# The row sum of two weight blocks, made by an adding DMA instead of VectorE, in a seven-product encoder layer

## The chip, the cores and the metric

The kernel runs on one core of a Trainium2 chip. The metric is the device time of one execution in microseconds: the median of three runs, 1981.27 us (1980.73 to 1982.22) for the kernel before. "Groups" below are the seven-product groups of the two large linear layers, and names such as B11 or T1 are the program's.

## The reference

One layer of an encoder over 512 tokens of width 2048, in float32:

```python
h = layer_norm(x, ln_in_g, ln_in_b)
z = h @ w_in
y = concat(attention(z), gelu(gate) * bidirectional_rg_lru(conv(z))) @ w_out
h = layer_norm(ALPHA * h + y, ln1_g, ln1_b)
f = square(relu(h @ w_up)) @ w_down          # 2048 -> 8192 -> 2048
h = layer_norm(ALPHA * h + f, ln2_g, ln2_b)
```

The change lies in the last two matrix products, `h @ w_up` and `... @ w_down`.

## The kernel before, in words

Every float32 operand is split into a high part (written as float32r by ScalarE, lines 121 and 159) and a low part (what is left, a subtraction on VectorE, lines 124 and 160). A product is then three matmuls: weight high by operand high, weight high by operand low, weight low by operand high.

The kernel goes through its stages in this order: the first norm and `w_in`, the attention and the recurrent branch, `w_out` with its norm, then `w_up` (from about 658 us on) and `w_down` (from about 1290 us on). For `w_up` and `w_down` the activations are cut into a 2x2 grid of blocks, and from the blocks seven operands are prepared once for a whole stage (B11, T3, T1, X4, B21, B22, T2), each with a high and a low part that stay in SBUF. The weights come as slabs of 128x1024 float32 (512 KB). Four slabs are the blocks a11, a12, a21, a22 of one group, and `winograd` (line 878) computes the group's four output blocks with seven block products instead of eight. The products run in the order B11, T3, T1, X4, B21, B22, T2, with 24 matmuls (3 for each of 8 slices) to each.

What the weights need ahead of a product: B11 takes a11, X4 takes a22 and B21 takes a12 as loaded; T3 takes a11-a21, T1 takes a21+a22, T2 takes a22 less that, and B22 takes a12 less T2's. These four sums are made by VectorE at line 876 (`tt`), each on 128x1024 float32 and each in place of one of its inputs. After that `wsplit` (line 839) makes the high part in one of three tiles `whi` and the low part in one of three tiles `wlo`.

The order of the instructions on each engine is set by a scheduler at build time, from the order in the program and its priorities: loads and splits are moved ahead of the products (the splits by `tc.high_priority`, line 841). Each engine then runs its own list in order. The loads are all issued by SyncE (SP) from one list; raw slabs go to seven buffers, of which the last four (`ws_p`, line 835) lie in space that is free only once the norm's rows R (`r_p`, freed at line 834) have been read for the last time, by the split of X4 in lines 826 to 833.

There are 57 groups: 30 in `w_up` (lines 924 to 936, after four blocks of 128 columns that are computed in the ordinary way) and 27 in `w_down` (lines 982 to 1016). `w_down` runs in four chunks, and at the end of `w_up` and of the first three chunks the operands of the next chunk are loaded from DRAM (`u_load`, line 912) and split; in between stands one block in the ordinary way (`classic`, line 760).

In the lists below, `raw` is a weight slab, `s` with a number the tiles s1 and s7, `st_mm`, `st_sc` and `st_tr` the PSUM banks of the products, `uo` an output tile of `w_up`, `R` the rows of a norm.

Of the kernel before, what the change touches and what calls it, by code (L numbers as in the profile page):

```python
# [9 lines left out]
F32 = mybir.dt.float32  # L10
# [3 lines left out]
ALU = mybir.AluOpType  # L14
# [4 lines left out]
P = 128  # L19
# [29 lines left out]
def body(tc, x, pos, vecs, consts, w_in, w_uq, w_kn, w_v, w_rg, w_out, w_up, w_down, out):  # L49
    nc = tc.nc  # L50
    V, A, T, G = nc.vector, nc.scalar, nc.tensor, nc.gpsimd
# [472 lines left out]
    for step, what in enumerate(ORDER):  # L524
        c, k = what[0], int(what[1])
# [309 lines left out]
    ws_p = pool("ws")  # L835
# [3 lines left out]
    def wsplit(f, n):  # L839
        woff[0] = (32, 0) if n in ("T3", "T1") else FAR  # L840
        with tc.high_priority(offset=PO2):
            w = wsplit_(f)
        woff[0] = FAR
        return w

    def wsplit_(f):
        hi = wtile(wr, "whi", 3)
        lon[0] += 1
        lo = wtile(wr, "wlo", 2) if lon[0] % 3 else wtile(ws_p, "wlo", 1)
        split(f, hi, lo)  # L850
        return hi, lo

    def wraw(k):
        if k % 7 < 3:
            return wr.tile([P, 1024], F32, tag="raw", name="raw", bufs=3)
        return ws_p.tile([P, 1024], F32, tag="raw", name="raw", bufs=4)
# [3 lines left out]
    def wload(src):  # L860
        t = wraw(rawn[0])
        rawn[0] += 1
        nc.sync.dma_start(out=t, in_=src)
        return t

    def product(acc, w, n, first):
        wh, wl = w
        sk = dict(skip_group_check=not first)
        for j in range(8):
            ws = slice(j * P, (j + 1) * P)  # L870
            T.matmul(acc, wh[:, ws], oph[n][:, j], start=first and j == 0, stop=False, **sk)  # L871
            T.matmul(acc, wh[:, ws], opl[n][:, j], start=False, stop=False, **sk)  # L872
            T.matmul(acc, wl[:, ws], oph[n][:, j], start=False, stop=j == 7, **sk)  # L873

    def tt(o, x, y, op):
        V.tensor_tensor(out=o, in0=x, in1=y, op=op)  # L876

    def winograd(slabs, evac, hook=lambda n: None):

        a11 = wload(slabs[0])  # L880
        a21 = wload(slabs[2])
        a22 = wload(slabs[3])
        a12 = wload(slabs[1])
        bank = lambda tag, bufs: ps.tile([P, HS], F32, tag=tag, name="st_" + tag, bufs=bufs)
        half = lambda n: ws_p.tile([P, HS], F32, tag=n, name=n, bufs=2)
        a, b, c, d = bank("mm", 3), bank("sc", 2), bank("tr", 3), bank("mm", 3)
        s1, s7 = half("s1"), half("s7")
        product(a, wsplit(a11, "B11"), "B11", True)
        hook("B11")
        A.activation(s1, a, AF.Copy)  # L890
        tt(a11, a11, a21, ALU.subtract)
        product(b, wsplit(a11, "T3"), "T3", True)
        A.activation(s7, b, AF.Copy)  # L893
        tt(a21, a21, a22, ALU.add)
        product(c, wsplit(a21, "T1"), "T1", True)
        tt(s7, s7, c, ALU.add)
        product(b, wsplit(a22, "X4"), "X4", False)
        hook("X4")
        tt(a11, a22, a11, ALU.subtract)
        product(a, wsplit(a12, "B21"), "B21", False)  # L900
        hook("B21")
        evac("c11", a, None)
        tt(a12, a12, a11, ALU.subtract)
        product(c, wsplit(a12, "B22"), "B22", False)
        hook("B22")
        product(d, wsplit(a11, "T2"), "T2", True)
        tt(s1, s1, d, ALU.add)
        evac("c21", s1, b)
        evac("c12", s1, c)
        evac("c22", s1, s7)  # L910
# [13 lines left out]
    for ch in range(NCL, DFF // 256):  # L924
        o = o_tile()

        def evac(which, x, y):
            t = o[:, 2 * int(which[1]) + int(which[2]) - 3, :]
            if y is not None:
                tt(t, x, y, ALU.add)  # L930
                x = t
            A.activation(t, x, AF.Relu)
            A.activation(t, t, AF.Square)
        winograd([w_up[4 * ch + i] for i in range(4)], evac,
                 *([next_ops(0)] if ch == DFF // 256 - 1 else ()))
        up_out(ch, o)
# [46 lines left out]
    for c in range(NCH):  # L983
        if c == 0:
            r_init(0)
        for i in range(KT // 2):
            sl = [w_down[(c * KT + 2 * i) * 2 + q] for q in range(4)]
            if c == NCH - 1 and i == KT // 2 - 1:
                last_pair(sl)
            elif i < NCL2:  # L990
                def evac(n, acc):
                    tt(r[2 * i + n], r[2 * i + n], acc, ALU.add)
                classic(sl, evac, [lambda n=n: u_load(c, n, n) for n in ("T3", "T1", "T2")] if i == 0 else ())
                if i == NCL2 - 1:
                    u_load(c, "T4", "X4")
            else:
                q = rp[i]

                def evac(which, x, y):
                    t = q[:, 2 * int(which[1]) + int(which[2]) - 3, :]  # L1000
                    if which == "c11":
                        tt(t, t, x, ALU.add)
                    elif which == "c22":
                        tt(y, y, x, ALU.add)
                        tt(t, t, y, ALU.add)
                    else:
                        tt(t, t, y, ALU.add)
                        tt(t, t, x, ALU.add)
                def prev_stats(n, i=i):
                    if n == "X4" and i == KT // 2 - 2:  # L1010
                        u_load(c, "B12", "X4")
                    if n == "B21":
                        for k in (2 * i - 2, 2 * i - 1):
                            to_tokens(r[k], st2, k)
                hook = () if c + 1 < NCH and i < KT // 2 - 1 else \
                    (next_ops(c + 1),) if c + 1 < NCH else (prev_stats,)
                winograd(sl, evac, *hook)
# [69 lines left out]
```

## Time and profile before

| | |
|---|---|
| median of three runs | 1981.27 us |
| the profiled execution | 1981.16 us |
| its span, from the first to the last instruction | 1979.4 us |
| mean granted TensorE clock | 0.998 |
| TensorE busy (matmul) | 1932.1 us, 98% |
| VectorE busy | 1501.8 us, 76% |
| ScalarE busy | 1014.6 us, 51% |
| GpSimd busy | 18.1 us, 1% |
| HBM | read 234.19 MB, written 46.14 MB |

The profiled execution is 0.11 us below the median, and 1.76 us of it lie outside its span. A busy share is an average over all stages; what limits one stage is read from the rows of that stage. "Idle before, releaser" tells how long an engine stood still ahead of an instruction, and which work ended last before it could start. The landing time of a DMA runs from its issue to its completion.

### The profile page before, as it was taken

How to read it: one execution, taken by the hardware profiler on the slowest of the kernel's cores; microseconds unless marked ns; L12 is line 12 of the kernel's file. 1: busy time of each engine (PE TensorE's matmuls, PEld its weight loads, DVE VectorE, ACT ScalarE, POOL GpSimd, SP SyncE). 2: the span in 40 equal slices, each digit the busy share in tenths (PEclk: the TensorE clock that was granted, in tenths of full speed). 3: DMA queues.
4: the chain of work that ended last, by engine and by line, in shares of the span. 5: the costliest groups of instructions: out<-in, count | busy, mean ns of one | idle time of the engine just before them, and what ended most of it. 6: DMA issues, size and time to landing. Idle time of an engine off the chain costs nothing.

```text
span 1979.4 us, 39294 instructions
## 1 busy us (share of the span) xinstructions
PE 1932.1 (98%) x16472; PEld 1899.7 (96%) x16472; DVE 1501.8 (76%) x2151; ACT 1014.6 (51%) x1479; POOL 18.1 (1%) x20
## 2 busy tenths in 40 slices
PE   6999999999999999999999999999999999999997
PEld 6999999888999999999999999999999999999997
DVE  7666655677433598888888888888898888888895
ACT  6565566555222455555555555566464454445453
POOL 1000000000000000000000000000000000000001
PEclk9999999999999999999999999999999999999999
DMA  7222222221333345454444445486364355347332
GB/s 244 96 96 94 91 93 85 65 59 65 107 107 123 115 150 204 156 180 154 179 159 162 176 156 182 153 295 223 118 222 162 107 185 198 109 140 244 100 104 86
DMA packets 113890, 284.19 MB, mean 144 GB/s; under 512 B 10161, under 2 KB 56369, under 8 KB 109617
## 3 DMA queue, kind: packets, MB, share of 16 engines
q1 hardware_dynamic: 113712, 281.68, 41.4%
q8 instruction: 129, 2.11, 0.4%
q14 instruction: 49, 0.39, 0.1%
HBM read 234.19 MB, written 46.14 MB: 142 GB/s over the span
## 4 chain that ended last, share of the span: by engine, by line
PE 88%; DVE 4%; ACT 3%; DMA 2%; issue 2%; POOL 0%; SPq 0%; ACTq 0%; DVEq 0%; POOLq 0%
PE st_mm L871 8%; PE st_mm L872 8%; PE st_mm L873 8%; PE mm L142 7%; PE mm L141 7%; PE mm L140 7%; PE st_tr L873 5%; PE st_sc L873 5%; PE st_sc L871 5%; PE st_tr L872 5%; PE st_tr L871 5%; PE st_sc L872 5%; PE mm L756 1%; PE mm L758 1%; PE mm L757 1%
## 5 line engine op out<-in xcount | busy, mean ns | idle before, releaser
L159 ACT ACTIVATE whi<-raw 128x1024 fp32r<-128x1024 f32 x399 | 423.5, 1063 | 513.5 <-DVE raw L876 251.6
L160 DVE TENSOR_TENSOR wlo<-raw,whi 128x1024 fp32r<-128x1024 f32 x399 | 484.5, 1222 | 129.4 <-ACT whi L159 123.5
L876 DVE TENSOR_TENSOR raw<-raw 128x1024 f32<-128x1024 f32 x228 | 278.3, 1221 | 3.6
L124 DVE TENSOR_TENSOR wlo<-raw,whi 128x1024 fp32r<-128x1024 f32 (+1 forms) x128 | 141.3, 1105 | 160.9 <-PE mm L142 110.3
L121 ACT ACTIVATE whi<-raw 128x1024 fp32r<-128x1024 f32 (+1 forms) x128 | 123.0, 966 | 195.6 <-PE mm L141 160.8
L141 PE MATMUL mm<-hl,whi 128*128 128x256 f32 x704 | 195.3, 277 | 0.0
L142 PE MATMUL mm<-hh,wlo 128*128 128x256 f32 x704 | 195.0, 277 | 0.0
L140 PE MATMUL mm<-hh,whi 128*128 128x256 f32 x704 | 194.7, 277 | 0.1
L140 PEld LDWEIGHTS mm<-hh,whi 128*128 128x128 f32 x704 | 132.2, 188 | 0.3 <-ACT xp L443 0.3
L142 PEld LDWEIGHTS mm<-hh,wlo 128*128 128x128 f32 x704 | 132.2, 188 | 0.1
L141 PEld LDWEIGHTS mm<-hl,whi 128*128 128x128 f32 x704 | 132.2, 188 | 0.0
L871 PE MATMUL st_sc<-X4h,whi 128*128 128x256 f32 x456 | 126.6, 278 | 2.0 <-ACT s L893 2.0
L873 PE MATMUL st_sc<-T3h,wlo 128*128 128x256 f32 x456 | 126.5, 277 | 1.8 <-DVE wlo L160 1.8
L871 PE MATMUL st_tr<-B22h,whi 128*128 128x256 f32 x456 | 126.6, 278 | 1.0 <-ACT whi L159 1.0
L873 PE MATMUL st_tr<-B22h,wlo 128*128 128x256 f32 x456 | 126.2, 277 | 0.7 <-DVE wlo L160 0.7
L871 PE MATMUL st_mm<-B21h,whi 128*128 128x256 f32 x456 | 126.0, 276 | 0.8 <-ACT s L890 0.8
L871 PE MATMUL st_mm<-T2h,whi 128*128 128x256 f32 x456 | 126.0, 276 | 0.4 <-ACT whi L159 0.4
L872 PE MATMUL st_sc<-X4l,whi 128*128 128x256 f32 x456 | 126.3, 277 | 0.0
L873 PE MATMUL st_sc<-X4h,wlo 128*128 128x256 f32 x456 | 126.2, 277 | 0.0
L871 PE MATMUL st_sc<-T3h,whi 128*128 128x256 f32 x456 | 126.1, 277 | 0.0
L872 PE MATMUL st_sc<-T3l,whi 128*128 128x256 f32 x456 | 126.1, 277 | 0.0
L873 PE MATMUL st_mm<-B11h,wlo 128*128 128x256 f32 x456 | 126.0, 276 | 0.0
(443 smaller groups left out, 6462.3 us busy)
## 6 DMA issues: line engine op xcount, KB each, us to landing
raw<-in_w_up SPq DMA_DIRECT2D x128, 512.0 KB, 3.3
raw<-in_w_down SPq DMA_DIRECT2D x128, 512.0 KB, 3.6
u_dram<-uo SPq DMA_DIRECT2D x32, 1024.0 KB, 3.8
raw<-in_w_in SPq DMA_DIRECT2D x50, 512.0 KB, 3.2
raw<-in_w_out SPq DMA_DIRECT2D x32, 512.0 KB, 3.2
X4l<-u_dram SPq DMA_DIRECT2D x18, 512.0 KB, 5.3
x<-in_x SPq DMA_DIRECT2D x8, 512.0 KB, 7.1
h_dram<-hf SPq DMA_DIRECT2D x32, 128.0 KB, 2.1
```

The source lines that it names most:

```text
L121: A.activation(hi[:, :w], raw[:, :w], AF.Copy)
L124: V.tensor_tensor(out=lo[:, :w], in0=raw[:, :w], in1=hi[:, :w].bitcast(F32), op=ALU.subtract)
L140: T.matmul(acc[:, c], wh, xh[:, c], start=first and t == 0, stop=False)
L141: T.matmul(acc[:, c], wh, xl[:, c], start=False, stop=False)
L142: T.matmul(acc[:, c], wl, xh[:, c], start=False, stop=last and t == 1)
L159: A.activation(hi, f, AF.Copy)
L160: V.tensor_tensor(out=lo, in0=f, in1=hi.bitcast(F32), op=ALU.subtract)
L756: T.matmul(o, wh[:, ws], oph[b][:, j], start=first and t == 0, stop=False)
L871: T.matmul(acc, wh[:, ws], oph[n][:, j], start=first and j == 0, stop=False, **sk)
L872: T.matmul(acc, wh[:, ws], opl[n][:, j], start=False, stop=False, **sk)
L873: T.matmul(acc, wl[:, ws], oph[n][:, j], start=False, stop=j == 7, **sk)
L876: V.tensor_tensor(out=o, in0=x, in1=y, op=op)
```

## The change

T1's sum a21+a22 is no longer made by VectorE. Each group gets a tile `s1w` of its own (two buffers, in `ws_p`): a plain DMA issued by SP loads a21 into it a second time, then an adding DMA issued by GpSimd (`accum_op=ALU.add`) adds a22 to it from DRAM. T1's split reads `s1w`. a21 and a22 are still loaded as before, for T3 and X4. The last line cuts the space that is kept for GpSimd's DMA descriptors to 8192 bytes a partition, which makes room for `s1w`.

```diff
@@ -881,6 +881,9 @@
         a21 = wload(slabs[2])
         a22 = wload(slabs[3])
         a12 = wload(slabs[1])
+        s1w = ws_p.tile([P, 1024], F32, tag="s1w", name="s1w", bufs=2)
+        nc.sync.dma_start(out=s1w, in_=slabs[2])
+        G.dma_start(out=s1w, in_=slabs[3], accum_op=ALU.add)
         bank = lambda tag, bufs: ps.tile([P, HS], F32, tag=tag, name="st_" + tag, bufs=bufs)
...
         A.activation(s7, b, AF.Copy)
-        tt(a21, a21, a22, ALU.add)
-        product(c, wsplit(a21, "T1"), "T1", True)
+        product(c, wsplit(s1w, "T1"), "T1", True)
@@ -1075,7 +1077,7 @@
-    nc = _bacc.Bacc("TRN2", target_bir_lowering=False, num_devices=1)
+    nc = _bacc.Bacc("TRN2", target_bir_lowering=False, num_devices=1, dynamic_dma_scratch_size=8192)
```

The scheduler lays the instructions out anew. Three places matter below.

SP's list of DMAs at the first group. Before (raw_8782, raw_8784, raw_8786 and raw_8788 are a11, a21, a22 and a12 of the first group, raw_9016 to raw_9022 those of the second):

```order
L863 DMA raw_8786<-in_w_up 128x1024
L777 DMA u_dram0_72<-uo_8307 128x2048
L863 DMA raw_8788<-in_w_up 128x1024
L863 DMA raw_9016<-in_w_up 128x1024
L863 DMA raw_9018<-in_w_up 128x1024
L863 DMA raw_9020<-in_w_up 128x1024
L863 DMA raw_9022<-in_w_up 128x1024
L863 DMA raw_9250<-in_w_up 128x1024
L777 DMA u_dram0_72<-uo_8308 128x2048
```

Now (raw_9018 to raw_9024 are the second group's, s1w_8790, s1w_9026 and s1w_9262 belong to the first, second and third group):

```order
L863 DMA raw_8786<-in_w_up 128x1024
L777 DMA u_dram0_72<-uo_8307 128x2048
L863 DMA raw_8788<-in_w_up 128x1024
L885 DMA s1w_8790<-in_w_up 128x1024
L863 DMA raw_9018<-in_w_up 128x1024
L863 DMA raw_9020<-in_w_up 128x1024
L777 DMA u_dram0_72<-uo_8308 128x2048
L863 DMA raw_9022<-in_w_up 128x1024
L863 DMA raw_9024<-in_w_up 128x1024
L885 DMA s1w_9026<-in_w_up 128x1024
L863 DMA raw_9254<-in_w_up 128x1024
L885 DMA s1w_9262<-in_w_up 128x1024
```

The first group's `s1w` stands right behind its a12, whose buffer is the first in `ws_p`, and ahead of the second group's slabs. On GpSimd, 57 adding DMAs stand in a row, one for each group, with nothing between them.

ScalarE's list at the first group. Before (whi_8826 is the high part for T3, whi_8856 that for T1, whi_8885 that for X4):

```order
L159 ACTIVATE whi_8826<-raw_8782 128x1024
L159 ACTIVATE whi_8856<-raw_8784 128x1024
L781 ACTIVATE uo_8308<-mm_8638 128x512
L782 ACTIVATE uo_8308<-uo_8308 128x512
L159 ACTIVATE whi_8885<-raw_8786 128x1024
L890 ACTIVATE s1_8794<-st_mm_8790 128x256
L159 ACTIVATE whi_8914<-raw_8788 128x1024
L893 ACTIVATE s7_8795<-st_sc_8791 128x256
```

Now (whi_8829 is the high part for T3, whi_8858 that for T1, whi_8887 that for X4):

```order
L159 ACTIVATE whi_8829<-raw_8782 128x1024
L781 ACTIVATE uo_8308<-mm_8638 128x512
L782 ACTIVATE uo_8308<-uo_8308 128x512
L893 ACTIVATE s1_8797<-st_mm_8793 128x256
L896 ACTIVATE s7_8798<-st_sc_8794 128x256
L159 ACTIVATE whi_8858<-s1w_8790 128x1024
L159 ACTIVATE whi_8887<-raw_8786 128x1024
L159 ACTIVATE whi_8916<-raw_8788 128x1024
```

T1's high part has moved behind the two copies of PSUM banks, and X4's and B21's high parts stand behind it.

TensorE's list where T1's product of the first group begins, now:

```order
L873 MATMUL st_sc<-T3h,wlo 128x256
L871 MATMUL st_tr<-T1h,whi 128x256
L872 MATMUL st_tr<-T1l,whi 128x256
L871 MATMUL st_sc<-X4h,whi 128x256
L872 MATMUL st_sc<-X4l,whi 128x256
L873 MATMUL st_tr<-T1h,wlo 128x256
L871 MATMUL st_tr<-T1h,whi 128x256
```

Before, X4's two matmuls stood behind all 24 of T1. This is the only place in the whole list of TensorE where the order has changed.

## Rows read from the trace of the kernel before

**Rows 1.** The page's busy times, and its group of VectorE's sums.

```profile
PE 1932.1 (98%) x16472; PEld 1899.7 (96%) x16472; DVE 1501.8 (76%) x2151; ACT 1014.6 (51%) x1479; POOL 18.1 (1%) x20
...
L876 DVE TENSOR_TENSOR raw<-raw 128x1024 f32<-128x1024 f32 x228 | 278.3, 1221 | 3.6
```

**Rows 2.** Busy time by stretch: w_up's groups, then the passage to w_down.

```profile
core 0: us, PE busy (x) PEld busy (x) DVE busy (x) ACT busy (x) POOL busy (x), PEclk, DMA share, GB/s
750.00:1298.00 548.00, 548.00 (x4828) 548.00 (x4827) 458.57 (x544) 297.31 (x483) 0.00 (x0) 1.00 0.47 167
1298.00:1326.00 28.00, 25.80 (x222) 25.19 (x221) 26.07 (x31) 23.30 (x31) 0.00 (x0) 1.00 1.01 351
```

**Rows 3.** TensorE's waits from 1298 to 1950: us in total, times, longest.

```profile
PE st_sc L871 <- ACT s L893: 2.0, 3, 1.2
PE st_sc L873 <- DVE wlo L160: 1.8, 2, 1.0
PE st_tr L871 <- ACT whi L159: 1.0, 1, 1.0
PE st_mm L871 <- ACT s L890: 0.8, 1, 0.8
PE st_tr L873 <- DVE wlo L160: 0.7, 2, 0.4
PE st_mm L871 <- ACT whi L159: 0.4, 1, 0.4
PE mm L758 <- DVE wlo L124: 0.3, 1, 0.3
```

**Rows 4.** VectorE in a later group: T1's low part.

```profile
1011.70 1.22 DVE L160 TENSOR_TENSOR wlo<-raw,whi 128x1024 fp32r<-128x1024 f32 x1
```

**Rows 5.** ScalarE in the group of rows 4: T1's high part.

```profile
1009.71 1.06 ACT L159 ACTIVATE whi<-raw 128x1024 fp32r<-128x1024 f32 x1 [0.65 <-PE st_mm L872]
```

**Rows 6.** ScalarE one group on: T1's high part.

```profile
1028.79 1.06 ACT L159 ACTIVATE whi<-raw 128x1024 fp32r<-128x1024 f32 x1 [0.65 <-PE st_mm L872]
```

**Rows 7.** Landing of all 228 loads of line 863.

```profile
DMA to landing us min/median/max: 3.0/3.3/9.1
```

**Rows 8.** VectorE in order of time: last read of R, first group's sums.

```profile
739.33 1.22 DVE L160 TENSOR_TENSOR X4l<-R,X4h 128x1024 fp32r<-128x1024 f32 x1
740.47 2.47 DVE L876 TENSOR_TENSOR raw<-raw 128x1024 f32<-128x1024 f32 x2
```

**Rows 9.** Line 863, issues at 740.6 and 741.0 us: first and last, their landing.

```profile
L863 SPq DMA_DIRECT2D raw<-in_w_up x2: 328/376/425, 740.6 to 741.0; - x2
...
DMA to landing us min/median/max: 3.7/4.1/4.6
```

**Rows 10.** ScalarE in order of time: T1's high part in the first group.

```profile
743.04 1.06 ACT L159 ACTIVATE whi<-raw 128x1024 fp32r<-128x1024 f32 x1 [0.25 <-DVE raw L876]
```

**Rows 11.** TensorE in order of time: T1's first matmul in the first group.

```profile
747.96 0.28 PE L871 MATMUL st_tr<-T1h,whi 128*128 128x256 f32 x1
```

**Rows 12.** GpSimd's groups: count, busy us and mean ns of one, idle before.

```profile
L409 POOL TENSOR_TENSOR sp_d<-sp_c,sp_b 128x16 f32<-128x16 f32 x1 | 2.9, 2930 | 1.9 <-DVE sp_b L406 1.9
L292 POOL TENSOR_TENSOR rsx<-vex,mhalf 128x1 f32<-128x1 f32 x4 | 2.2, 552 | 31.0 <-DVE vex L290 23.6 <-DVE sp_d L417 7.4
```

**Rows 13.** Landing of line 863's load issued at 745.4 us.

```profile
DMA to landing us min/median/max: 5.3/5.3/5.3
```

**Rows 14.** Landing of line 777's store of 1 MB issued at 749.0 us.

```profile
DMA to landing us min/median/max: 7.6/7.6/7.6
```

**Rows 15.** TensorE near the end: the first matmul after a wait.

```profile
1967.77 0.47 PE L217 MATMUL trb<-ident,R 128*128 128x128 f32 x1 [3.54 <-ACT R L199]
```

**Rows 16.** Stretches of 1 us near the end, columns as in rows 2.

```profile
1966.00:1967.00 1.00, 0.00 (x0) 0.00 (x0) 0.29 (x2) 0.09 (x1) 0.90 (x2) 0.69 0.00 0
1967.00:1968.00 1.00, 0.23 (x1) 0.23 (x2) 1.00 (x3) 0.72 (x1) 1.00 (x1) 0.50 0.00 0
...
1972.00:1973.00 1.00, 1.00 (x6) 0.75 (x4) 0.69 (x2) 0.62 (x2) 1.00 (x1) 0.50 0.75 263
1973.00:1974.00 1.00, 0.24 (x2) 0.12 (x2) 0.76 (x2) 0.56 (x1) 0.23 (x1) 0.89 0.75 262
```

## The prediction

> **What bounds the kernel now.** I began with the page's busy times: TensorE works for 98% of the span and VectorE for 76% [rows 1]. That is an average, so the next view is the table by stretch. In the 548 us of `w_up`'s groups TensorE is busy for all 548.00 us, while VectorE works 458.57 us, 84% [rows 2]. In that stretch no work taken off VectorE can end anything sooner; TensorE's list sets the time. The reader should look for the places where TensorE does wait. From 1298 to 1950 us there are 7.0 us of waits in seven rows [rows 3], nearly all where `w_down`'s chunks change: there the DMA share stands at 1.01 and the granted clock at 1.00 [rows 2]. Only three of these rows, 1.8 + 0.7 + 0.3 = 2.8 us, end with work of VectorE [rows 3]. So the change can win at most a few microseconds, and the question is what its new chain costs where the chain has no lead.
>
> **What is removed.** One of four sums per group: 57 of the 228 sums of 1221 ns, 69.6 us of VectorE [rows 1]. In the groups of `w_up` it lies beside a TensorE that never waits: worth nothing. At the changes of chunk it can be worth at most the 2.8 us that end on VectorE. I take 0: in those 28 us ScalarE is busy 23.30 and the DMA share is 1.01 [rows 2], so when VectorE comes sooner, ScalarE or a landing is late next.
>
> **What is added.** Per group one plain load of 512 KB from SP and one adding DMA of 512 KB from GpSimd. VectorE's sum had no load of its own; the new chain is load, then adding DMA, then T1's split. There are two buffers `s1w`, so a group's load can start when T1's split of two groups before is done.
>
> In the running state that is early enough. T1's low part ends at 1011.70 + 1.22 = 1012.92 us [rows 4]; T1's high part comes every 1028.79 - 1009.71 = 19.08 us [rows 6, 5], so two groups on it is due at 1047.87. That leaves 34.9 us for load and addition. A load lands in 3.3 us at the median and 9.1 at the longest [rows 7]. Even two of the longest fit, with 16 us to spare: cost 0. Behind GpSimd's wait nothing is queued but the next group's addition, and on SP the load's wait for the split two groups back has passed before its turn. The traffic grows from a DMA share of 0.47 [rows 2] by two more transfers of 512 KB on the six such units of a group (four slabs and a 1 MB store), or three if the adding one also reads its destination: 0.47 x 8/6 = 0.63 to 0.47 x 9/6 = 0.71, below 1.
>
> In the first group there is no lead. `s1w` lies in the space of R, which VectorE reads until 739.33 + 1.22 = 740.55 us [rows 8]. SP can issue only then; before, it issued a12 at 740.6 and the next slab at 741.0, and that second one landed 4.6 us later, at 745.6 [rows 9]. In the new order that second place is `s1w`'s. Before, T1's sum was one of two made from 740.47 on [rows 8], its high part began at 743.04 [rows 10], and TensorE reached T1 at 747.96 [rows 11].
>
> Now the addition starts at 745.6 at the earliest. No row shows an adding DMA or a DMA from GpSimd, so it is bounded. Below: GpSimd takes no time and the transfer is the shortest load, 3.0 us [rows 7]: sum ready at L = 748.6. Above: GpSimd takes its longest instruction, 2.9 us [rows 12], and the transfer the longest load, 9.1 us [rows 7]: L = 757.6. A gain is excluded, since T1 had its inputs in time before. Nearest are the transfers issued in this same crowded stretch: a load of 512 KB took 5.3 us [rows 13], a store of 1 MB 7.6 us [rows 14]. The adding DMA writes 512 KB but must also read both addends, so I take a value between them, 6.4 us, and 0.6 us for GpSimd, its short instruction [rows 12]: L = 745.6 + 0.6 + 6.4 = 752.6.
>
> From L on: the high part, 1.06 us [rows 10], then the low part, 1.22 us [rows 4]; so all of T1 can run from L + 2.28. ScalarE's X4 split is queued behind T1's, so X4 cannot fill the gap. TensorE's new order lets four matmuls go early; each takes 548.00/4828 = 0.113 us [rows 2], 0.45 in all. TensorE loses L + 2.28 - 747.96 - 0.45 = L - 746.13: **6.5 us** at my L, 2.5 and 11.5 at the ends. After it TensorE is the bound again, so nothing gives this back. The second group's sum has the same chain but is due 19.08 us later, plus the loss; its load is issued behind the 1 MB store, which was issued at 749.0 and landed at 756.6 [rows 14]; a load and an addition of 3.3 us each would end at 763.2, and T1's split is due at 743.04 + 19.08 + 6.5 = 768.6 [rows 5, 6, 10].
>
> **The clock.** Near the end TensorE waits 3.54 us until 1967.77 [rows 15]. The granted clock falls to 0.69 in the microsecond before and stands at 0.50, the 1.2 GHz level, until 1973, when it is 0.89 [rows 16]. From 1967.77 to 1973.1 that is 5.3 us at half speed, a loss of 2.7 us. The wait in the first group would be 752.6 + 1.06 - 747.96 = 5.7 us, longer than this one. I add **2.7 us**; the lower end is 0, if the wait turns out short.
>
> **The passages.** At the later changes of chunk one `s1w` load stands between two operand loads. At 351 GB/s [rows 2] its 512 KB take 1.5 us, three times, 4.5 us if all of it reached TensorE. The operand loaded there is X4, the fourth of the next group's products, so I take 0. The shift of SBUF addresses has no row that prices it; the matmuls of all seven products run at one rate, so I take 0.
>
> **Sum.** 0 + 6.5 + 2.7 + 0 = +9.2 us on the profiled 1981.16 gives 1990.4. That execution lies 0.11 below the median of the runs, so against the median the forecast is **1990.5 us**, +0.46%. A measurement of this kernel can tell about 0.2% from no change, which is 4.0 us.
>
> **Rivals.** The wait is short: no change. If the addition lands like the shortest load, L = 748.6, TensorE loses 2.5 us, its wait is 748.6 + 1.06 - 747.96 = 1.7 us, shorter than the one near the end, and I leave the clock's price out: 1983.8. For it: the median load is 3.3 us [rows 7]. Against it: every transfer issued at this moment took 3.7 us or more [rows 9, 13, 14]. The Trainium skill, page "DMA: Bandwidth & Descriptors", section "Anatomy of one DMA — SWDGE (gpsimd) path", prices a DMA from GpSimd at about 2.0 us plus bytes / 436e3; my estimate from it is 3.2 us for 512 KB, with which the sum would be +2.7 us, this rival's side. No run here shows such a DMA yet. Chance 0.26.
>
> The passages gain: faster. If VectorE's shorter list pulls the work that ends all the waits at the changes of chunk forward, 7.0 us go [rows 3]; with the short wait the net is 2.5 - 7.0 = -4.5 us, 1976.8. It decides only if more than 2.5 + 4.0 = 6.5 of the 7.0 us vanish. Against it: only 2.8 us of them end on VectorE. Chance 0.05.
>
> Every group is late: much slower. If load and addition take longer than 34.9 us, T1 waits in each of the 57 groups: each microsecond over is 57 us, 2038 at the first. Nothing in the rows comes near; only the unknown speed of the addition speaks for it. Chance 0.07.
>
> The passages lose. The 4.5 us above on top of the forecast: 1995.0. Chance 0.04.
>
> That VectorE keeps the sum can be excluded: its list has one sum less in each group, and the adding DMAs stand on GpSimd's.
>
> **How the numbers follow.** The forecast itself (a wait of more than 4 us net, in the first group) gets 0.58. Slower is this, every group late and the passages losing: 0.58 + 0.07 + 0.04 = 0.69. Within 0.2% is the short wait, 0.26; faster 0.05. The range begins at 1982.0, the short wait's 1983.8 with 1.8 us of VectorE's waits gone [rows 3], and ends at 1997.0, the upper L with the clock, 1981.3 + 11.5 + 2.7 = 1995.5, and one passage's 1.5 us. Left out are every group late and most of the gain: some 0.12, with the tails under 0.2.
>
> **What would show it.** Right: in the first group a wait of TensorE ahead of T1's first matmul of some 5.7 us (near 748 to 754), which ends with ScalarE's high part and behind it the adding DMA; some microseconds of granted clock 0.50 after it; TensorE busy again in all of the rest of `w_up`; VectorE's sums at 171 instead of 228. Wrong: a landing of the first addition before 750.2 us, where the loss falls to 4 us; a wait ahead of T1 in later groups; a stretch from 1298 on with clearly fewer or more waits than 7.0 us; no fall of the clock.

## The result and the profile after

The changed kernel takes **2002.53 us** (median of four runs, 2001.94 to 2003.18) where the kernel before takes 1981.54 on the same chip: ratio 1.0097, 95% interval 1.0085 to 1.0109, 21 us slower. The forecast was 1990.5, range 1982.0 to 1997.0: the right side and less than half of the size. The profiled execution has a span of 2000.2 us, 20.8 more than before.

The page of the changed kernel: busy times of the engines, VectorE's sums, and the two DMA queues (packets, MB, share of 16 engines' span; q1 is SP's, q0 is GpSimd's).

```profile
PE 1939.1 (97%) x16472; PEld 1905.9 (95%) x16472; DVE 1447.9 (72%) x2094; ACT 1015.2 (51%) x1479; POOL 68.1 (3%) x77
...
L876 DVE TENSOR_TENSOR raw<-raw 128x1024 f32<-128x1024 f32 x171 | 209.0, 1222 | 4.2
...
q1 hardware_dynamic: 121920, 311.57, 45.2%
q0 software_dynamic: 8208, 29.89, 9.1%
```

VectorE has lost its 57 sums (228 to 171, [rows 1]) and TensorE works as many matmuls as before, 7 us longer. Where did 21 us go? The start of each group's first matmul (B11) in the two traces, taken group by group (counted from 0), gives it: the difference grows in three places and is nearly flat between them. I call that growth, between a group's start and the next one's, the **loss** of the group:

| place | near | loss, us |
|---|---|---|
| group 0, the first of `w_up` | 748 | 11.1 |
| groups 1 to 28 | 772 to 1306 | 0.0 |
| group 31, the second behind the passage to `w_down` | 1378 | 4.9 |
| group 51, the first behind the last change of chunk | 1834 | 5.2 |
| all the rest together (most of it: group 37, +0.8, and group 30, -0.4) | | 0.2 |

TensorE's time line of the changed kernel at the three places; the bracket is the wait ahead of the matmul and what ended it.

```profile
755.48 0.58 PE L871 MATMUL st_tr<-T1h,whi 128*128 128x256 f32 x1 [7.80 <-ACT whi L159]
...
1378.18 0.38 PE L871 MATMUL st_tr<-T1h,whi 128*128 128x256 f32 x1 [2.24 <-ACT whi L159]
...
1834.06 0.58 PE L873 MATMUL st_sc<-T3h,wlo 128*128 128x256 f32 x1 [3.32 <-DVE wlo L160]
```

**The first group** went as forecast in kind. GpSimd's first adding DMA starts as soon as the plain load has landed, and ScalarE's high part waits for it (GpSimd's and ScalarE's time lines, then the landing of that DMA and, in the last line, of all 57):

```profile
745.63 1.08 POOL L886 DMA_DIRECT2D s1w<-in_w_up  x1 [47.95 <-DMA raw<-in_w_up]
...
754.37 1.06 ACT L159 ACTIVATE whi<-s1w 128x1024 fp32r<-128x1024 f32 x1 [6.27 <-DMA s1w<-in_w_up]
...
DMA to landing us min/median/max: 8.7/8.7/8.7
...
DMA to landing us min/median/max: 5.4/6.0/9.8
```

It started at 745.63 (745.6 in the forecast) and landed at 754.3 (752.6 in the forecast). Stretches of 1 us from TensorE's wait on, columns as in [rows 2], show the clock:

```profile
750.00:751.00 1.00, 0.00 (x0) 0.00 (x0) 0.00 (x0) 0.00 (x0) 0.00 (x0) 0.90 0.86 180
751.00:752.00 1.00, 0.00 (x0) 0.00 (x0) 0.00 (x0) 0.00 (x0) 0.00 (x0) 0.50 1.03 201
...
761.00:762.00 1.00, 1.00 (x11) 1.00 (x10) 0.28 (x1) 0.35 (x1) 0.00 (x0) 0.98 0.93 254
```

From 751 to 761 the granted clock is 0.50 (1.2 GHz). TensorE is back at work at 755.48, so some 5.6 us of its work run at half speed, which costs 2.8 us. The trace counts a matmul as busy for 0.28 us, while they follow each other every 0.11 us, so a wait costs some 0.17 us more than its bracket. With a second wait, of 0.15 us, behind the first that gives some 7.97 + 0.32 + 2.8 = 11.1, the loss of this group.

**Group 31** was not in the forecast. ScalarE's time line shows why T1's high part is late there:

```profile
1375.24 1.94 ACT L953 ACTIVATE R<-R 128x512 f32<-128x512 f32 x3 [5.45 <-DMA R<-h_dram]
1377.09 1.04 ACT L159 ACTIVATE whi<-s1w 128x1024 fp32r<-128x1024 f32 x1
```

`s1w` itself was ready long before: its adding DMA was issued at 1361.08 and landed 5.6 us later, at 1366.7; that of group 32 was issued at 1364.77 and landed at 1374.6. In ScalarE's list T1's high part stands behind three scalings of rows R that are being loaded for `w_down` (`r_init`), and these wait for their loads. The three loads in question landed in this time after their issue (first two lines; the last two are the loads of R issued at this point before):

```profile
L952 SPq DMA_DIRECT2D R<-h_dram x3: 431/489/931, 1365.8 to 1367.3; - x3
...
DMA to landing us min/median/max: 9.2/9.4/9.6
...
L950 SPq DMA_DIRECT2D R<-h_dram x6: 430/431/435, 1355.2 to 1357.5; - x6
...
DMA to landing us min/median/max: 4.4/6.0/6.3
```

Before, T1's high part was made ahead of need.

**Group 51** waits for T3's low part. VectorE makes it behind X4's low part, whose operand comes from DRAM (VectorE's time line, then TensorE's wait at the same place in the kernel before):

```profile
1831.64 1.23 DVE L160 TENSOR_TENSOR X4l<-X4l,X4h 128x1024 fp32r<-128x1024 f32 x1 [1.42 <-ACT X4h L159]
1832.79 1.22 DVE L160 TENSOR_TENSOR wlo<-raw,whi 128x1024 fp32r<-128x1024 f32 x1
...
1815.75 0.39 PE L873 MATMUL st_sc<-T3h,wlo 128*128 128x256 f32 x1 [0.75 <-DVE wlo L160]
```

In SP's list the load of group 52's `s1w` now stands between the two loads of X4; before, a slab stood there, which now stands ahead of both. The second load of X4 lands 8.2 us after its issue (first two lines) instead of 5.6 (last two):

```profile
L919 SPq DMA_DIRECT2D X4l<-u_dram x1: 377/377/377, 1822.3 to 1822.3; - x1
...
DMA to landing us min/median/max: 8.2/8.2/8.2
...
L917 SPq DMA_DIRECT2D X4l<-u_dram x1: 377/377/377, 1806.5 to 1806.5; - x1
...
DMA to landing us min/median/max: 5.6/5.6/5.6
```

TensorE's waits of the stretch of [rows 3], in the changed kernel (taken to 1970, as it runs some 20 us later):

```profile
PE st_sc L873 <- DVE wlo L160: 4.0, 2, 3.3
PE st_tr L871 <- ACT whi L159: 3.0, 2, 2.2
PE st_sc L871 <- ACT s L896: 2.2, 3, 1.2
PE st_tr L873 <- DVE wlo L160: 1.9, 3, 0.8
PE st_mm L871 <- ACT s L893: 0.8, 1, 0.8
PE st_mm L871 <- ACT whi L159: 0.4, 1, 0.4
PE mm L758 <- DVE wlo L124: 0.3, 1, 0.3
```

They sum to 12.6 us instead of 7.0. So of the 10.1 us that groups 31 and 51 lose, somewhat more than half is waits. The granted clock falls with each of the two, to 0.50 from 1378.8 to 1382.3 and from 1832.8 to 1839.7, which makes the rest (stretches within these two):

```profile
1379.00:1382.00 3.00, 2.56 (x12) 2.56 (x13) 2.95 (x6) 3.00 (x7) 0.00 (x0) 0.50 0.53 179
1834.00:1839.00 5.00, 4.94 (x23) 4.95 (x24) 4.01 (x5) 0.01 (x1) 0.00 (x0) 0.50 0.39 120
```

### The profile page after: what moved, and what is told of

It reads as the page before. It is cut to its first block, busy times and chain, and to the rows that moved or that the text cites. A ratio compares the mean times of both kernels' runs of the same rounds, so it can differ in the third digit from the quotient of the medians.

```text
span 2000.2 us, 39534 instructions
## 1 busy us (share of the span) xinstructions
PE 1939.1 (97%) x16472; PEld 1905.9 (95%) x16472; DVE 1447.9 (72%) x2094; ACT 1015.2 (51%) x1479; POOL 68.1 (3%) x77
## 3 DMA queue, kind: packets, MB, share of 16 engines
q0 software_dynamic: 8208, 29.89, 9.1%
## 4 chain that ended last, share of the span: by engine, by line
PE 85%; DVE 5%; DMA 4%; ACT 4%; issue 2%; POOL 0%; SPq 0%; ACTq 0%; DVEq 0%; POOLq 0%
PE st_mm L871 7%; PE st_mm L872 7%; PE st_mm L873 7%; PE mm L142 7%; PE mm L141 7%; PE mm L140 7%; PE st_tr L873 5%; PE st_sc L871 5%; PE st_sc L873 5%; PE st_tr L871 5%; PE st_tr L872 5%; PE st_sc L872 5%; PE mm L758 1%; PE mm L757 1%; PE mm L756 1%
## 5 line engine op out<-in xcount | busy, mean ns | idle before, releaser
L159 ACT ACTIVATE whi<-raw 128x1024 fp32r<-128x1024 f32 x342 | 359.8, 1061 | 478.2 <-DVE raw L876 249.7
L160 DVE TENSOR_TENSOR wlo<-raw,whi 128x1024 fp32r<-128x1024 f32 x342 | 415.1, 1222 | 179.7 <-ACT whi L159 173.1
L876 DVE TENSOR_TENSOR raw<-raw 128x1024 f32<-128x1024 f32 x171 | 209.0, 1222 | 4.2
L871 PE MATMUL st_tr<-T1h,whi 128*128 128x256 f32 x456 | 127.9, 280 | 10.0 <-ACT whi L159 10.0
L873 PE MATMUL st_tr<-T1h,wlo 128*128 128x256 f32 x456 | 128.0, 281 | 1.3 <-DVE wlo L160 1.3
L872 PE MATMUL st_tr<-T1l,whi 128*128 128x256 f32 x456 | 127.5, 280 | 0.0
```

Of the source, the lines that this page charges most:

```text
L159: A.activation(hi, f, AF.Copy)
L160: V.tensor_tensor(out=lo, in0=f, in1=hi.bitcast(F32), op=ALU.subtract)
```

## The experiments

**Theory A**: three separate losses; in the first group the chain load, addition, split starts too late, in groups 31 and 51 the extra traffic makes *other* loads land late on which ScalarE's and VectorE's lists hang, and the clock falls with each wait. **Rivals**: a cost in every group (addresses, smaller descriptor space, traffic), or the chain being late everywhere. All were timed against the kernel before, run on the same chip. The losses come from each profiled execution, against the trace of before; what stages ahead of group 0 differ by is left out. They are single executions: in ten of the runs group 29, at the passage to `w_down`, takes some 2 us longer than in the trace of before, in e1 too, where nothing is changed behind group 0. The clock falls there for 3.5 us, and in the trace of before it does not. So a loss of some 2 us in one of these groups does not by itself show an effect of the DMA.

| run | ratio, 95% interval | group 0 | group 1 | group 31 | group 51 |
|---|---|---|---|---|---|
| the change | 1.0097 (1.0085 to 1.0109) | 11.1 | 0.0 | 4.9 | 5.2 |
| e1_first_only | 1.0050 (1.0030 to 1.0071) | 11.1 | 0.0 | 0.2 | 0.6 |
| e2_not_first | 1.0030 (1.0019 to 1.0041) | 0.0 | 0.0 | 3.2 | 3.7 |
| e3_steady_only | 0.9997 (0.9985 to 1.0009) | 0.0 | 0.0 | 0.0 | 0.0 |
| e4_traffic_only | 1.0689 (1.0661 to 1.0716) | 0.0 | 0.0 | 0.0 | 0.4 |
| e5_load_only | 1.0001 (0.9992 to 1.0010) | 0.0 | 0.0 | 0.0 | 0.3 |
| e6_plain_from_gpsimd | 1.0064 (1.0047 to 1.0081) | 9.4 | 0.0 | 1.7 | 0.7 |
| e7_in_place | 1.0523 (1.0506 to 1.0540) | 8.8 | 1.8 | 7.0 | -0.2 |
| e8_fill | 1.0094 (1.0074 to 1.0113) | 11.8 | 0.0 | 3.5 | 5.0 |
| e9_first_early | 1.0034 (1.0021 to 1.0047) | 0.0 | 4.0 | 2.4 | 0.7 |
| e10_no_32_52 | 1.0078 (1.0059 to 1.0097) | 11.7 | 0.0 | 0.5 | 3.4 |
| e11_fill80 | 1.0079 (1.0062 to 1.0096) | 9.9 | 0.0 | 4.7 | 1.0 |
| e12_traffic_read | 1.0024 (1.0014 to 1.0035) | 1.1 | 0.0 | 2.3 | -0.2 |
| e13_fifty | 1.0019 (1.0009 to 1.0028) | 0.0 | 0.4 | 1.6 | -0.3 |
| e14_change_again | 1.0100 (1.0084 to 1.0117) | 11.0 | 0.0 | 3.6 | 1.8 |
| e15_plain_again | 1.0070 (1.0055 to 1.0086) | 9.0 | 0.0 | 2.5 | 1.0 |

### Where the loss lies: e1, e2, e3

One condition on the group's number decides who makes T1's sum; `by_dma` is `grp[0] == 0` in e1, `grp[0] > 0` in e2, and in e3 it leaves out group 0 and, around each change of chunk, the last group before and the first two behind it.

```diff
+        grp[0] += 1
+        by_dma = grp[0] == 0
+        if by_dma:
+            s1w = ws_p.tile([P, 1024], F32, tag="s1w", name="s1w", bufs=2)
+            nc.sync.dma_start(out=s1w, in_=slabs[2])
+            G.dma_start(out=s1w, in_=slabs[3], accum_op=ALU.add)
...
-        product(c, wsplit(s1w, "T1"), "T1", True)
+        if not by_dma:
+            tt(a21, a21, a22, ALU.add)
+        product(c, wsplit(s1w if by_dma else a21, "T1"), "T1", True)
```

> Only the first group's T1 sum is made by the adding DMA; the other 56 groups use VectorE's sum. Theory A (three separate places: the first group's chain, and two groups behind changes of chunk where extra traffic makes other loads land late): the first group's loss alone, +11 us on before (1992.5, ratio 1.0055), TensorE waits 7 to 8 us ahead of T1 near 748 us and then runs at granted clock 0.50 until about 762; no new wait after 1298 us. Rival (a cost of every group or of the moved SBUF addresses): with one group of 57 changed, the loss is under 2 us or does not depend on the group.

> All groups but the first use the adding DMA. Theory A: the first group's 11 us are gone and the changes of chunk keep their loss, +8 to +11 us on before (1989.5 to 1992.5), with T1 or T3 waits of 2 to 4 us near 1367 and 1823 us and a fall of the granted clock after each. Rival (the second group inherits the first one's missing lead): a wait of several us ahead of T1 in the second group, near 767 us.

> The adding DMA is used only in groups that lie away from the first group and from the changes of chunk (44 of 57). Theory A: 1981.5, within 1 us of before, although VectorE still loses 44 sums of 1.22 us and the DMA traffic of those groups is that of the changed kernel. Rival (the moved SBUF addresses, the smaller descriptor space or the steady traffic cost time): slower by 5 us or more.

e1 loses 11.1 us in the one group it changes, with TensorE's wait at the same place:

```profile
757.14 0.58 PE L871 MATMUL st_tr<-T1h,whi 128*128 128x256 f32 x1 [8.19 <-ACT whi L159]
```

e2 loses 3.2 and 3.7 in groups 31 and 51 and nothing in its second group; by its ratio it is 6 us slower, under the 8 to 11 expected. e3 is the plainest: 44 groups with the adding DMA, and no difference. Its stretch in the midst of `w_up`, and that of the kernel before below it:

```profile
780.00:1290.00 510.00, 510.00 (x4493) 510.00 (x4492) 401.73 (x483) 279.33 (x457) 23.60 (x27) 1.00 0.70 221
```

```profile
780.00:1290.00 510.00, 510.00 (x4493) 510.00 (x4492) 428.33 (x511) 278.18 (x456) 0.00 (x0) 1.00 0.47 166
```

VectorE works 27 us less, the DMA share goes from 0.47 to 0.70, and TensorE has 510.00 of 510 us in both. In the running state the sum is worth nothing on VectorE and costs nothing as a DMA; the rivals with a cost in every group fall, the moved addresses among them.

### The first group: e9, e8, e11

e9 moves the first group's `s1w` out of the space of R:

```diff
         a21 = wload(slabs[2])
+        if grp[0] == 0:
+            s1w = wload(slabs[2])
         a22 = wload(slabs[3])
         a12 = wload(slabs[1])
-        s1w = ws_p.tile([P, 1024], F32, tag="s1w", name="s1w", bufs=2)
-        nc.sync.dma_start(out=s1w, in_=slabs[2])
+        if grp[0] > 0:
+            s1w = ws_p.tile([P, 1024], F32, tag="s1w", name="s1w", bufs=2)
+            nc.sync.dma_start(out=s1w, in_=slabs[2])
         G.dma_start(out=s1w, in_=slabs[3], accum_op=ALU.add)
```

> The change, but the first group's s1w takes the third of the buffers that are free before R is (where a22 stood), so its load is issued with the earliest slabs; a22 and a12, wanted later, move into the space of R. Theory A (the first group loses because its load has to wait for R's space): TensorE's wait ahead of T1 goes from 7.8 to under 1 us, the granted clock stays at 1.00 from 750 to 762, the total falls by 10 to 12 us, to +8 to +11 on before, what is left being the two groups behind the changes of chunk. Rival (the adding DMA in the crowd is late wherever its load stands): a wait of 3 us or more stays ahead of T1 or of X4.

The first group loses 0.0 us, with the same load, the same addition and the same split. The total falls to +7 us by the ratio, a little under the +8 to +11 expected, and two parts of that went otherwise: the second group waits (0.86, 0.76 and 1.50 us) and loses 4.0, and group 51 loses only 0.7. The second group's `s1w` is the first to lie in R's space in e2 too, where nothing is lost; but here its load is issued 3.4 us later, behind one more slab and a store, and its addition lands 5.0 us later, counted from the start of the first group. The clock stays at 1.00 in both groups. That the chain has no lead, since its load waits for R's space, is shown.

e8 and e11 keep the chain and give TensorE work to do instead of waiting:

```diff
+        wt3 = wsplit(a11, "T3")
+        product(b, wt3, "T3", True)
...
+        if grp[0] == 0:
+            for j in range(64):
+                T.matmul(c, wt3[0][:, :P], oph["T3"][:, j % 8], start=j == 0, stop=j == 63, skip_group_check=True)
         product(c, wsplit(s1w, "T1"), "T1", True)
```

> The change, with 64 matmuls of no use (T3's operand by T3's weights into T1's bank, overwritten by T1's first product) put ahead of T1 in the first group, so that TensorE works while it would wait. Theory A (part of the loss is the granted clock that falls after the wait): no fall of the clock at 750 to 762 us; the first group's loss goes from 11.1 to 8 to 9 us and the total is 2 to 3.5 us under the changed kernel. Rival (the clock falls for another reason or costs nothing here): the clock still falls, or the time is that of the change or longer.

> As e8_fill with 80 matmuls of no use instead of 64 (9.1 us instead of 7.3), so that they reach to where T1's parts are ready. Theory A (the clock falls after a wait of TensorE): no stretch of granted clock under 1.00 between 745 and 765, and the first group's loss is the 9.1 us and at most 1.5 us of wait. Rival (the clock falls whatever TensorE does there): a stretch of 0.50 remains and the loss is 12 us or more.

e8 missed: the first addition took 9.8 us to land instead of 8.7, so T1's parts came later than in the change; TensorE still waited 1.65 and 0.81 us behind the 64 matmuls, and the clock fell after that, for some 3.5 us instead of 10.3 (between 759 and 763, columns as in [rows 2]):

```profile
757.31 0.38 PE L871 MATMUL st_tr<-T1h,whi 128*128 128x256 f32 x1 [1.65 <-ACT whi L159]
...
759.00:760.00 1.00, 1.00 (x8) 1.00 (x7) 1.00 (x2) 0.15 (x1) 0.73 (x1) 0.67 0.00 0
...
762.00:763.00 1.00, 1.00 (x7) 1.00 (x7) 0.05 (x2) 0.11 (x1) 0.00 (x0) 0.63 1.00 221
```

Its loss of 11.8 us is the matmuls, the waits and the clock together, no gain. e11, with 80, waits 0.59 us in all, and the clock is 1.00 throughout:

```profile
755.00:765.00 10.00, 9.40 (x83) 9.24 (x83) 4.37 (x4) 2.96 (x3) 0.89 (x1) 1.00 0.74 224
```

Its loss is 9.9 us (9.1 of matmuls, 0.6 of waiting), 1.2 less than the change. So here the fall follows from TensorE's standing still, as forecast, and its price is the half-speed work behind the wait.

### Groups 31 and 51: e10, e13, e14, e5, e6, e15

> The change, with VectorE's sum in two groups only, counted from 0: 32 and 52, whose plain loads and adding DMA are issued while the loads that group 31 and group 51 wait for are on their way. Theory A: the losses of groups 31 and 51 (together 8 to 10 us) go, the first group's 11 us stay: +10 to +13 on before. Rival (the adding DMAs of all groups delay those loads): 18 us or more stay.

With `by_dma` as `grp[0] not in (32, 52)`, group 31's loss goes from 4.9 to 0.5. In ScalarE's list only one scaling of R, not three, now stands ahead of T1's high part. Its load was issued with no adding DMA in flight and took 6.1 us (ScalarE's time line, then that load):

```profile
1375.14 0.64 ACT L960 ACTIVATE R<-R 128x512 f32<-128x512 f32 x1 [2.04 <-DMA R<-h_dram]
1375.68 1.05 ACT L159 ACTIVATE whi<-s1w 128x1024 fp32r<-128x1024 f32 x1
...
L959 SPq DMA_DIRECT2D R<-h_dram x1: 422/422/422, 1369.1 to 1369.1; - x1
...
DMA to landing us min/median/max: 6.1/6.1/6.1
```

6.1 us instead of 9.4: the adding DMA of group 32, which nothing needs for more than 20 us, delays R, R delays ScalarE's scalings, and these hold T1's split. What the shorter row of scalings gives beside that was not tested apart. In e13 below, where group 32 keeps VectorE's sum too, group 31 loses 1.6, against 2.3 to 4.9 in the seven runs that issue group 32's addition near these loads (the change, e2, e8, e9, e11, e12, e14). Half of the expectation missed: group 51 kept 3.4 us, because the scheduler had put group 53's load of `s1w` into the place of group 52's, between the two loads of X4.

> The adding DMA in 50 of the 57 groups: VectorE's sum in groups 0, 32 and 52 to 56, so that no load of s1w stands between the two loads of X4 ahead of group 51 (the slab that the change puts ahead of them stays there). Theory A (the loss of group 51 is the second X4 load landing behind an s1w load): T3's wait in group 51 falls from 3.3 to under 1.2 us and the granted clock stays at 1.00 there; the total is that of before within 2 us, but for 2 to 4 us that the second group may lose. Rival (the slab that now stands ahead of X4 is what delays it): a wait of 2 us or more stays in group 51.

> The change itself once more, on the chip of the other runs of this call. Theory A: the same three losses, 11 us in the first group, 3 to 5 us in group 31, 3 to 5 us in group 51; +17 to +21 us on before. Rival (the loss of group 51 comes and goes between executions, whatever the DMA does): under 1.5 us in group 51.

e13's condition is `grp[0] not in (0, 32) and grp[0] < 52`; in its list for SP the slab still stands ahead of X4's loads and no `s1w` between them. Its wait in group 51:

```profile
1819.72 0.39 PE L873 MATMUL st_sc<-T3h,wlo 128*128 128x256 f32 x1 [0.44 <-DVE wlo L160]
```

0.44 instead of 3.32, so the rival (the slab) falls. Across the runs the wait goes with the landing of X4's second load. Counted from the start of group 51's first matmul, it lands at -0.44 in e13, +0.28 before, +0.99 in e9, +2.07 in e14 and +2.85 in the change; the waits are 0.44, 0.75, 1.46, 2.54 and 3.32, from the second on 0.47 more than the landing. e14, the change once more, waits 2.54 us and loses only 1.8, since here the clock does not fall; in e10, after a wait of 2.67, it does, and the loss is 3.4. In all nine runs with a load of `s1w` between X4's loads (the change, e2, e6, e8, e9, e10, e11, e14, e15) the wait is 1.46 to 3.32 us, in the eight without one 0.44 to 1.35. So the load in between lengthens the wait, by how much varies from run to run, and where the clock falls that nearly doubles it. The total of e14 is that of the change again. e13 itself comes out at 1.0019: with the adding DMA in 50 groups most of the loss is gone and nothing is won.

> T1 takes VectorE's sum as before; the plain load of s1w is still issued in all groups, the adding DMA is left out. Theory A1 (the adding DMA holds the DMA engines about twice as long per byte as a plain one and is what delays the loads at the changes of chunk): most of that loss goes, +0 to +4 us on before. Theory A2 (the plain loads that stand in SP's list between the operand loads are what delays them): the loss at the changes of chunk stays, +6 to +10 us.

> The GpSimd DMA stays in its place and its chain but writes a22 instead of adding it, so T1's product is computed from a22 alone (a21 is left out of the sum). Theory A1 (adding costs about twice the DMA time per byte): the first GpSimd DMA lands in 4.5 to 6.5 us instead of 8.7, TensorE's wait ahead of T1 falls from 7.8 to 4 to 6 us, the share of the GpSimd queue falls from 9.1% to about 4.5%, total +4 to +10 us on before. Rival (a DMA from GpSimd is slow whatever it does): landing 8 us or more and a total as with the change, +20 to +22 us.

> The kernel of e6_plain_from_gpsimd once more (T1's product is computed from a22 alone). In e6 group 51 lost only 0.7 us, with SP's list as in the change. If the adding decides that loss, it is again under 1.5 us here; if the landing of X4 varies by itself between executions, it may be 2 to 4 us here.

```diff
-        G.dma_start(out=s1w, in_=slabs[3], accum_op=ALU.add)
+        G.dma_start(out=s1w, in_=slabs[3])
```

(e6 and e15; e5 leaves the line out and keeps VectorE's sum.) With the plain load alone (e5) nothing is lost, as A1 had it, but e5 does not test it: nothing reads its `s1w`, so the scheduler pulled these loads ahead, and the last of the 57 was issued at 927 us. For groups 31 and 51 it says nothing. e6 and e15 show what the adding adds, since SP, ScalarE and VectorE have the same lists there as in the change. The same 29.89 MB take 4.8% of the DMA engines' time instead of 9.1%:

```profile
q0 software_dynamic: 8208, 29.89, 4.8%
```

The loads of R issued behind it around the start of group 31 land in 6.3 to 7.7 us in e6 and e15, against 8.3 to 9.6 behind an adding one in the change and e14; group 31 loses 1.7 and 2.5 us, against 4.9 and 3.6. That the plain one delays R too is not shown: with no DMA from GpSimd in flight such loads took 3.8 to 7.2 us (before, e1, e3, e4, e5, e10, e13). The first DMA from GpSimd, however, still takes long in its crowd, and over all 57 the times are (first line the first one, second line all):

```profile
DMA to landing us min/median/max: 7.7/7.7/7.7
...
DMA to landing us min/median/max: 3.5/4.8/7.8
```

I had expected 4.5 to 6.5 us for the first. In e15 it took 7.0, while the first adding one took 8.6 to 9.8 in the six runs that keep its chain (the change, e1, e8, e10, e11, e14). So of the first landing only some 1 to 3 us are the adding; the rest is a transfer issued behind the burst of slabs, and in e6 TensorE still waits 6.96 us. Group 51 lost 0.7 and 1.0 us in e6 and e15, but the runs that add and have the same load between X4's lie between 0.7 (e9) and 5.2, so this tells nothing of the adding, of which none is in flight there. Why the landing of X4 behind the same load varies by some 2 us between runs is left open.

### Three other ways to place the work: e4, e12, e7

> T1 takes VectorE's sum as before, while the plain load and the adding DMA are still issued in all 57 groups and read by nothing. Theory A: the first group's chain is gone (its T1 wait falls from 7.8 to under 2 us), the losses at the changes of chunk stay since they come from traffic, +6 to +11 us on before. Rival (the chain load, addition, split is what is late everywhere): 1981.5, no loss at all.

```diff
-        product(c, wsplit(s1w, "T1"), "T1", True)
+        tt(a21, a21, a22, ALU.add)
+        product(c, wsplit(a21, "T1"), "T1", True)
```

This missed both expectations: 137 us slower, all in groups 3 to 13. SP's time line shows what happened:

```profile
785.49 1.53 SPq L863 DMA_DIRECT2D raw<-in_w_up  x1
787.11 19.58 SPq L885 DMA_DIRECT2D s1w<-in_w_up  x3
806.79 0.96 SPq L863 DMA_DIRECT2D raw<-in_w_up  x2
```

With no reader of `s1w` the scheduler pulled its loads far ahead; three of them stand in a row on SP, each waiting for the addition two groups back, and the slabs queue behind them for 20 us. TensorE then waits up to 24 us. In the change it is T1's split, as the reader, that keeps these loads in their place. e12 gives `s1w` a small reader behind T1's product:

```diff
+        tt(s1w[:, :1], s1w[:, :1], s7[:, :1], ALU.add)
```

> As e4_traffic_only, T1 takes VectorE's sum and both DMAs are still issued, but one small VectorE instruction behind T1's product reads s1w, so that its load cannot run ahead as it did there. Theory A (e4's +137 us came from plain loads of s1w that ran ahead in SP's list and held the slabs behind them): the +137 us are gone, the total is 0 to +8 us on before, with no wait over 2 us in the first group. Rival (the traffic of the adding DMA is too much for every group): waits in most groups of w_up, +50 us or more.

+5 us by the ratio, as theory A had it: the full traffic without the chain costs 1.1 us in group 0 and 2.3 in group 31. In group 51 it costs nothing; there no load of `s1w` stands between X4's loads.

> The adding DMA adds a22 from DRAM into a21's own buffer after T3's sum has read it; no second load of a21 and no tile s1w. Theory A: the first group's chain starts at 741.7 us instead of 745.6, so TensorE's wait ahead of T1 falls from 7.8 to 2 to 5 us (loss 2 to 7 us with the clock), and half of the extra transfers at the changes of chunk are gone; total +3 to +12 us. Rival (the adding DMA's traffic alone makes the loss at the changes of chunk): that loss stays as with the change, about 10 us.

Against the kernel before:

```diff
-        tt(a21, a21, a22, ALU.add)
+        G.dma_start(out=a21, in_=slabs[3], accum_op=ALU.add)
         product(c, wsplit(a21, "T1"), "T1", True)
...
```

I had looked at the first group alone and missed the mechanism: in every group of `w_up` the addition can begin only when T3's sum has read a21, and its landing plus the split comes too late. ScalarE's wait in one group, and the sums of TensorE's waits from 790 to 1290, 24 groups:

```profile
985.75 1.06 ACT L159 ACTIVATE whi<-raw 128x1024 fp32r<-128x1024 f32 x1 [5.17 <-DMA raw<-in_w_up]
...
PE st_tr L873 <- DVE wlo L160: 18.2, 24, 0.8
PE st_sc L871 <- ACT s L893: 5.2, 24, 0.2
PE st_tr L871 <- ACT whi L159: 2.7, 3, 1.4
```

Each group of `w_up` loses some 1.5 us or more, most of `w_down` about 1, 104 us in all. This is the rival "every group is late" of the forecast, made real by taking the lead away; the second tile `s1w` with its 34.9 us is what the change pays a second load of a21 for.

No variant is faster than the kernel before.

## Why the prediction was right or wrong

- **TensorE bounds `w_up`, so the removed sums are worth 0: right.** e3 takes 44 of them away and stays at 0.9997.
- **Load and addition hide in the running state: right.** Groups 1 to 28 lose 0.0 us. The DMA share there is 0.70, inside the forecast's 0.63 to 0.71, at the end with three transfers; in e6, which does not add, it is 0.64.
- **First group, +6.5 and +2.7 us: right in mechanism, too small.** Measured 11.1. The addition landed in 8.7 us, not in 0.6 + 6.4 = 7.0, inside the stated bounds (L = 754.3 between 748.6 and 757.6): 1.7 us more, and the prediction's own L - 746.13 then gives 8.2. The clock cost 2.8 instead of 2.7; that it agrees to a tenth is luck, for by the same reckoning it is 2.0 to 3.1 in e1, e10 and e14. e9 shows the missing lead, e11 the clock.
- **The passages, "I take 0": this is the step that failed.** Groups 31 and 51 lost 10.1 us (5.4 in e14). The step named X4's loads alone, and R's do not occur in it. It asked where X4 stands among TensorE's products and found it late, the fourth. It did not ask what stands behind X4's and R's loads in VectorE's and ScalarE's lists: T3's and T1's splits, the next products to come. It also priced the traffic by bytes at 351 GB/s (1.5 us for an `s1w`), which left out the adding DMA altogether; R's loads took 3 to 5 us longer. And its bound of 4.5 us had no term for the clock, though the text had just priced that for the first group; of the 4.5 the range took in one 1.5, and so ended at 1997.0. The prediction's own sign of being wrong, clearly more waits than 7.0 us from 1298 on, came: 12.6.
- **Rivals.** The short wait is out: the adding DMA takes 5.4 us at the least and 6.0 at the median, the plain one of e6 3.5 and 4.8. The estimate from the Trainium skill's formula (page "DMA: Bandwidth & Descriptors", section "Anatomy of one DMA — SWDGE (gpsimd) path") was 3.2 us, less than any of these. "The passages lose", at a chance of 0.04, came true on top of the forecast, but with 10.1 us instead of 4.5, half of it through R's loads, which it did not have.

## What to carry to other kernels

Work taken off an engine that is not the bound was worth nothing here, but the transfers put in its place can still cost: look for the places where loads already run at full share, and for each load that comes later there, read the in-order lists of the engines behind it, because the instruction that is held up may be for another product altogether. A new chain of load, addition and split needs its lead in every place where it starts, the first group above all; and a wait of a few microseconds on TensorE should be priced with the half-speed clock that may follow it.

## What the runs showed of the hardware

- An adding DMA from DRAM into SBUF holds the DMA engines about twice as long for its bytes as a plain one: 9.1% of the span for 29.89 MB, against 4.8% for the same DMAs without the addition. It lands in 6.0 us at the median instead of 4.8, and issuing it keeps GpSimd 0.87 us instead of 0.54. The Trainium skill, page "Collectives: The Full Stack", section "The bandwidth ceiling: the fold count and why AG ≠ RS ≠ AR", says of reduce-scatter that it is slower than all-gather not for the cycles of its add but because the add needs two source reads. The factor here, 9.1 / 4.8 = 1.9, is of the size that a second read would give; no run here shows the reads themselves.
- Loads from SP that are issued behind it land later: loads of R around the start of group 31 in 8.3 to 9.6 us (the change, e14), in 6.3 to 7.7 behind a plain DMA of the same size with the same lists (e6, e15).
- The granted clock fell to 0.50 for 3.5 to 10.3 us with some of TensorE's waits, and the length of the wait alone did not decide it: after 1.65 and 0.81 us it fell (e8), after 2.54 us it did not (e14).
